# Summing four half rows with one product: the ada rows of a two-block transformer kernel

## The chip, the cores and the metric

The kernel runs on one core of a Trainium2 chip. The metric is the device time of one execution in microseconds (us), lower is better. The engines are named as in the profile: PE is TensorE's matmul, PEld its weight load, DVE is VectorE, ACT is ScalarE, POOL is GpSimd and SP is SyncE, which here issues nearly all DMA transfers; "SPq" marks its queue. A transfer is carried out by 16 DMA engines, which cut it into packets.

## What is computed

The reference runs two transformer blocks over 512 tokens of width 1024. What matters here is the second block's conditioning, computed once for each of its two layers, and the first block's feed-forward part, during which the kernel computes it:

```
def hybrid_layer_2(x, c_act, positions, norm_w, w_ada, b_ada, w_in, ...):
    mod = c_act @ w_ada + b_ada                 # (1,1024) @ (1024,3072)
    shift, scale, gate = jnp.split(mod, 3, axis=-1)
    h = rmsnorm(x, norm_w) * (1.0 + scale[:, None, :]) + shift[:, None, :]
    ...
    return x + gate[:, None, :] * (merged @ w_out)

def second_block(x, c, ...):
    c_act = jax.nn.silu(c)
    ...
def hybrid_layer(x, ...):                        # the first block's end
    ...
    f_gate, f_up = jnp.split(hf @ w_ffn_in, 2, axis=-1)
    f = (jax.nn.silu(f_gate) * f_up) @ w_ffn_out
    return x + rms_norm(f, g_post_ffn)
```

So six rows of 1024 numbers are wanted, three for each layer: shift, scale and gate. Each is a product of one vector with a matrix of 1024 x 1024; all six weight matrices together are 25 MB.

## The kernel before

The large products are made in pairs of fp32r numbers: a weight tile `wr` (128x1024, 512 KB) is loaded by SP (L191, two buffers), ACT rounds it to `wh` (L144), DVE subtracts to get the rest `wl` (L145), each in four buffers and a fifth from another pool, and PE makes three products for each 128 rows: high with high, high with low, low with high. A weight tile of the feed-forward stage (FFN) gives 24 products of 128x128 with 128x512.

The FFN's first half has 44 such tiles. `F_many` makes the first five in halves of 256 tokens and the other 39 whole; I call these 39 the full tiles. After each tile, `done(i, ps)` turns PSUM into `f`: for even i a tanh on ACT and a product on DVE (`ft`, L755), for odd i a product (L759) and a split into high and low (L147 on ACT, L148 on DVE).

The ada rows are computed beside this. `done` starts the generator `ada` when i is 0. A row of 1024 is made as two half rows of 512, so there are twelve half rows. For each one:
- DVE clears an accumulator `acc` (128x512, L573) and SP loads the half row of `b_ada` into its first partition (L574);
- eight times, SP loads a weight tile `aw`: 128 rows of 512 numbers, 256 KB, five buffers (L577), and DVE adds `aw` times a column of `cact` to `acc` (L578). `cact` holds the conditioning vector after silu, 128 numbers in each of eight columns;
- ACT and DVE split `acc` into high and low (L144, L145), and PE sums over the partitions with two products against a 128x128 matrix of ones (`onesr`);
- ACT copies the first row of the result, adding 1.0 for the scale rows (L586), and SP stores it to `ada_rows` in device memory (L587).

The generator yields the time after which its next step is due, by a clock of the program's own that counts PE's products; `tick` in `F_` takes the next step of the generator whose due time has passed. So the pace, 1.2 per `aw` tile, decides where the steps stand among the FFN's products. Within `load_w` a higher priority moves the steps of the weight tiles ahead. In the end each engine has one fixed order, and each works through its own in order. `next_norm` reads two of the rows later, when the second block's normalisation is prepared.

Of the kernel before, what the change touches and what calls it, by code (L numbers as in the profile page):

```python
# [7 lines left out]
F32 = mybir.dt.float32  # L8
F32R = mybir.dt.float32r
I32 = mybir.dt.int32  # L10
AF = mybir.ActivationFunctionType
ALU = mybir.AluOpType
# [3 lines left out]
P = 128  # L16
# [34 lines left out]
class Block:  # L51
# [313 lines left out]
    def run(self):  # L365
        tc, nc, A = self.tc, self.nc, self.A
        with ExitStack() as es:
            self.es = es
            pool = lambda name, **kw: es.enter_context(tc.tile_pool(name=name, bufs=kw.pop("bufs", 1), **kw))
            self.cp = pool("const")  # L370
            self.smp = pool("small", bufs=12)
            self.es_ps = None
            self.psum(ps=8)
            self.hp = pool("h")
            self.dp = pool("dram", space=bass.MemoryType.DRAM)
            self.ident = self.cp.tile([P, P], F32, name="ident")
            self.ones = self.cp.tile([P, P], F32, tag="ones", name="ones")
            self.eps = self.cp.tile([P, 1], F32, tag="eps", name="eps")
            nc.vector.memset(self.eps, EPS)
            nc.scalar.activation(self.sm(), self.eps, AF.Sqrt)  # L380
            nc.vector.memset(self.ones, 1.0)
            self.cact = self.cp.tile([P, 8], F32, tag="cact", name="cact")
            self.xd = [self.dp.tile([S, D], F32, tag=f"xd{i}", name=f"xd{i}") for i in range(3)]
            self.block2(*self.block1())
            self.es_ps.close()
# [168 lines left out]
        v.tensor_add(self.merged[i], self.merged[i], T)  # L554


    def ada_init(self):
        nc, A = self.nc, self.A
        c = self.const("c_2")
        nc.scalar.activation(self.cact, c, AF.Tanh, scale=0.5)  # L560
        nc.vector.scalar_tensor_tensor(self.cact, self.cact, 1.0, c, op0=ALU.add, op1=ALU.mult)
        nc.vector.tensor_scalar(self.cact, self.cact, 0.5, None, op0=ALU.mult)
        self.ada_rows = self.dp.tile([6, D], F32, tag="adar", name="adar")

    def ada(self, pool, pace):

        nc, A, v = self.nc, self.A, self.nc.vector
        ones = pool.tile([P, P], F32R, tag="ones", name="onesr")
        nc.scalar.activation(ones, self.ones, AF.Copy)
        for l, j in [(l, j) for l in range(2) for j in range(6)]:  # L570
            o = slice(j * 512, j * 512 + 512)
            acc = pool.tile([P, 512], F32, tag="acc", name=self.nm("acc"), bufs=2)
            v.memset(acc, 0.0)  # L573
            nc.sync.dma_start(out=acc[0:1, :], in_=A["b_ada_2"][l:l + 1, o])  # L574
            for k in range(8):
                w = pool.tile([P, 512], F32, tag="aw", name=self.nm("aw"), bufs=5)
                nc.sync.dma_start(out=w, in_=A["w_ada_2"][l, k * P:(k + 1) * P, o])  # L577
                v.scalar_tensor_tensor(acc, w, self.cact[:, k:k + 1], acc, op0=ALU.mult, op1=ALU.add)  # L578
                yield pace
            hi, lo = (pool.tile([P, 512], F32R, tag="acc" + c, name=self.nm("acc"), bufs=1) for c in "hl")  # L580
            self.split(hi, lo, acc)
            yield 7.0
            ps = self.pst()
            self.mm(ps, ones, hi, True, False)
            self.mm(ps, ones, lo, False, True)
            nc.scalar.activation(acc[0:1], ps[0:1], AF.Copy, bias=1.0 if j // 2 == 1 else 0.0)  # L586
            nc.sync.dma_start(out=self.ada_rows[l * 3 + j // 2:l * 3 + j // 2 + 1, (j % 2) * 512:(j % 2) * 512 + 512], in_=acc[0:1])  # L587


    def rnn_init(self):  # L590
# [148 lines left out]
    def ffn(self, hf, fp, es_w):  # L739
        tc, nc, A, v = self.tc, self.nc, self.A, self.nc.vector  # L740
        f, th = [], {}
        es = ExitStack()
        pool = []

        def done(i, ps):
            if i == 0:
                self.wait()
                es_w.close()
                pool.append(es.enter_context(tc.tile_pool(name="ffnt", bufs=1, side="right", reuse_waits="tile")))
                self.ada_init()  # L750
                self.spawn(self.ada(pool[0], 1.2))
            if i % 2 == 0:
                t = pool[0].tile([P, S], F32, tag="ft", name=self.nm("ft"), bufs=3)
                nc.scalar.activation(t, ps, AF.Tanh, scale=0.5)
                v.scalar_tensor_tensor(t, t, 1.0, ps, op0=ALU.add, op1=ALU.mult)  # L755
                th[0] = t
            else:
                t = th[0]
                v.tensor_mul(t, t, ps)  # L759
                ft_ = fp.tile([P, 2, S], F32R, tag="f", name=self.nm("f"), bufs=22)  # L760
                self.split(ft_[:, 0, :], ft_[:, 1, :], t, scale=0.5)
                f.append(ft_)

        self.F_many(hf, [A["w_ffn_in"][j * 22 + i] for i in range(22) for j in range(2)], done, halves=5)
        self.wait()
        es.close()
        flat = lambda: fp.tile([P, 2, S], F32R, tag="f", name=self.nm("f"), bufs=22).rearrange("p a q -> p (a q)")
        return lambda k, t, lo: f[k][:, lo, t * P:(t + 1) * P], lambda: [(flat(), flat()) for _ in range(4)]


    def next_norm(self, l, op, pool):

        nc, A, v = self.nc, self.A, self.nc.vector
        if l == 2:
            fin = self.row(A["final_norm_w_2"], pool, "amul")

            halves = []

            def first(t, x):

                xn = pool.tile([P, D], F32, tag="xn", name=self.nm("xn"), bufs=4)
                ms = self.sm()
                nc.scalar.activation(xn[:, :512], x[:, :512], AF.Square, scale=1.0 / 32.0, accum_out=ms)
                v.tensor_mul(xn[:, :512], x[:, :512], fin[:, :512])
                halves.append((xn, self.plus_eps(ms)))

            def more(t, x, a, b):

                xn, e = halves[t]
                ms = self.sm()  # L790
                nc.scalar.activation(xn[:, a:b], x[:, a:b], AF.Square, scale=1.0 / 32.0, accum_out=ms)
                if b < D:
                    v.tensor_mul(xn[:, a:b], x[:, a:b], fin[:, a:b])
                    e2 = self.sm(2)[:, :1]
                    v.tensor_add(e2, e, ms)
                    halves[t] = xn, e2
                    return
                r = self.rsqrt_act(ms, e)
                o = self.out[t * P:(t + 1) * P, :]
                v.scalar_tensor_tensor(xn[:, a:], x[:, a:], r, fin[:, a:], op0=ALU.mult, op1=ALU.mult)  # L800
                nc.sync.dma_start(out=o[:, a:], in_=xn[:, a:])
                nc.scalar.activation(xn[:, :a], xn[:, :a], AF.Copy, scale=r)
                nc.scalar.dma_start(out=o[:, :a], in_=xn[:, :a])

            def last(t, x):
                more(t, x, 512, D)
                yield 0.0

            last.more = more
            last.first = first  # L810
            return last
        nw = self.row(A["norm_w_2"][l], pool, "xn", bufs=2)
        am = self.row(self.ada_rows[l * 3 + 1], pool, "amul")
        sh = self.row(self.ada_rows[l * 3], pool, "ashift")
        v.tensor_mul(am, am, nw)

        def cb(t, x):
            nc.sync.dma_start(out=self.xd[l + 1][t * P:(t + 1) * P, :], in_=x)
            yield from self.norm_T(x, t, op, am, pool, shift=sh, lag=2.0)

        return cb
# [718 lines left out]
def cols(vec, n=None):  # L1540

    return np.ascontiguousarray(vec.reshape(-1, P).T)


def prep(inp):

    f = np.float32
    I = {k: np.asarray(a) for k, a in inp.items()}
    o = {}
    w = I["w_in"][0]  # L1550
# [3 lines left out]
    i = np.arange(P)  # L1554
    m = np.zeros((P, 512), f)
# [3 lines left out]
    n = np.arange(32)  # L1559
# [21 lines left out]
    rows = [cw[0], cw[1], cw[2], cw[3], I["rnn_conv_b"][0], I["rnn_ba"][0], I["rnn_bx"][0], I["rnn_lam"][0]]  # L1581
    o["rnn_cols"] = np.ascontiguousarray(np.stack([cols(r) for r in rows], 1))
    rw = np.zeros((8, P, 2, P), f)
    for j, nme in enumerate(("rnn_wa", "rnn_wx")):
        for h in range(16):
            q = (h % 2) * 64
# [36 lines left out]
    o["w2_out"] = np.stack([packT(I["w_out_2"][l]) for l in range(2)])  # L1623
    o["norm_w_2"], o["final_norm_w_2"] = I["norm_w_2"], I["final_norm_w_2"]
    o["ret_gn"] = np.stack([cols(I["ret_gn_w_2"][l]) for l in range(2)])
    o["c_2"] = cols(I["c_2"][0])
    o["w_ada_2"], o["b_ada_2"] = I["w_ada_2"], I["b_ada_2"]
    w2 = I["nsa_wk2"][0].reshape(2, P, 64).transpose(1, 0, 2)
    o["nsa_wk2"] = np.ascontiguousarray(np.concatenate([w2, w2], 2))
# [24 lines left out]
```

## Time and profile before

| what | before |
|---|---|
| time, median of 3 runs | 2517.1 us (2516.03 to 2517.49) |
| the profiled execution | 2515.06 us |
| its span, first to last instruction | 2513.3 us |
| PE busy | 2493.3 us, 99% of the span |
| DVE busy | 1403.6 us, 56% |
| ACT busy | 1062.7 us, 42% |
| DMA, mean rate over the span | 114 GB/s |
| `aw` loads | 96 of 256 KB, 3.9 us from issue to landing |

The rows come from one profiled execution. A busy row gives time, share of the span and number of instructions. Rows of the timeline give the start, the time and the number of instructions in a row; PE's products overlap, so the step from one start to the next is what one costs. Waits are put down to what came last. In the DMA view, packets under 512 B are counted apart.

### The profile page before, as it was taken

The page shows a single profiled execution, that of the slowest core. Times are in us where ns is not written, and L with a number is a line of the kernel's source. Part 1 is how long each engine was busy: PE and PEld are TensorE (multiplying, and loading weights), DVE is VectorE, ACT ScalarE, POOL GpSimd, SP SyncE. Part 2 cuts the span into 40 slices and gives each one's busy share as a digit, 9 for nine tenths or more (in the row PEclk, how much of TensorE's full clock was granted, in tenths as well). Part 3 has the DMA queues.
Part 4 walks back from the last instruction along what each step waited for, and adds up shares of the span by engine and source line. Part 5 has one row for each costly group of instructions (what it writes and reads, how often), then busy time and mean ns, then how long its engine had stood idle before and what let it go on. Part 6 is the DMA issues. An engine that isn't in the chain of part 4 may idle for free.

```text
span 2513.3 us, 31228 instructions
## 1 busy us (share of the span) xinstructions
PE 2493.3 (99%) x11850; PEld 2056.5 (82%) x11850; DVE 1403.6 (56%) x2651; ACT 1062.7 (42%) x1829; POOL 99.2 (4%) x104
## 2 busy tenths in 40 slices
PE   9999999999999999999999999999999999999998
PEld 7877777878888888888888888888888888888887
DVE  6567665776656777626333436664452343375635
ACT  4477666875334333324343432323233334233323
POOL 0023332000000000000000000000000000000000
PEclk9999999999999999999999999999999999999999
DMA  5522222323345666534422122222443222322233
GB/s 181 173 80 78 70 71 93 95 88 110 118 131 182 211 194 216 184 132 142 134 93 92 62 90 82 86 76 92 144 141 126 89 79 68 101 70 98 68 100 118
DMA packets 99129, 286.47 MB, mean 114 GB/s; under 512 B 13193, under 2 KB 19209, under 8 KB 98850
## 3 DMA queue, kind: packets, MB, share of 16 engines
q1 hardware_dynamic: 98256, 283.22, 35.2%
q8 instruction: 93, 1.52, 0.3%
q10 hardware_dynamic: 722, 1.25, 0.1%
q14 instruction: 58, 0.48, 0.1%
HBM read 259.16 MB, written 12.61 MB: 108 GB/s over the span
## 4 chain that ended last, share of the span: by engine, by line
PE 92%; DVE 3%; ACT 2%; DMA 2%; issue 1%; POOL 0%; ACTq 0%; POOLq 0%; DVEq 0%
PE ps L129 89%; PE ps L138 3%; DMA wr<-in_w_out_dram 1%; DVE wl L145 1%; ACT S L1416 1%; ACT wh L144 0%; DMA wr<-in_w_o_dram 0%; DVE yr L145 0%; POOL S L1423 0%; DVE PTl L145 0%; DVE S L1410 0%; ACT S L1421 0%; DMA x<-in_x_dram 0%; DVE xc L629 0%; DMA wr<-in_nsa_wv_dram 0%
## 5 line engine op out<-in xcount | busy, mean ns | idle before, releaser
L129 PE MATMUL ps<-h,wh 128*128 128x512 f32 (+1 forms) x4000 | 1242.8, 391 | 0.0
L129 PEld LDWEIGHTS ps<-h,wh 128*128 128x128 f32 x4000 | 733.5, 188 | 139.3 <-issue 5.1
L145 DVE TENSOR_TENSOR wl<-wr,wh 128x1024 fp32r<-128x1024 f32 x383 | 469.1, 1225 | 556.1 <-ACT wh L144 555.2
L144 ACT ACTIVATE wh<-wr 128x1024 fp32r<-128x1024 f32 x383 | 405.6, 1059 | 871.4 <-PE ps L129 658.3
L129 PE MATMUL ps<-h,wl 128*128 128x512 f32 (+1 forms) x2000 | 772.9, 386 | 0.0
L129 PEld LDWEIGHTS ps<-h,wl 128*128 128x128 f32 x2000 | 375.9, 188 | 75.7 <-DVE wl L145 0.4
L129 PE MATMUL ps<-wh,h 128*128 128x512 f32 x832 | 261.2, 392 | 0.3 <-ACT h L144 0.3
L129 PEld LDWEIGHTS ps<-wh,h 128*128 128x128 f32 x832 | 156.6, 188 | 33.6 <-DVE h L145 0.8
L129 PE MATMUL ps<-wl,h 128*128 128x512 f32 x416 | 162.4, 390 | 0.0
L129 PE MATMUL ps<-y,wh 128*128 128x512 f32 x384 | 119.3, 391 | 0.0
L129 PEld LDWEIGHTS ps<-wl,h 128*128 128x128 f32 x416 | 78.4, 188 | 16.1
L129 PE MATMUL ps<-wh,f 128*128 128x512 f32 x288 | 89.6, 389 | 0.0
L129 PEld LDWEIGHTS ps<-y,wh 128*128 128x128 f32 x384 | 71.5, 188 | 14.4
L129 PE MATMUL ps<-yr,wh 128*128 128x512 f32 x256 | 78.8, 389 | 0.0
L1416 ACT ACTIVATE S<-S,sm 128x128 f32<-128x128 f32 (+3 forms) x128 | 70.2, 550 | 19.0 <-DVE sm L1414 18.8
L1423 POOL TENSOR_SCALAR S<-S,sm 128x128 f32<-128x128 f32 (+3 forms) x64 | 69.6, 1099 | 214.0 <-ACT Q L144 78.2
L145 DVE TENSOR_TENSOR PTl<-ps,PTh 128x512 fp32r<-128x512 f32 (+1 forms) x96 | 65.0, 683 | 22.4 <-ACT PTh L144 21.6
L144 ACT ACTIVATE PTh<-ps 128x512 fp32r<-128x512 f32 (+1 forms) x96 | 56.1, 588 | 49.0 <-PE ps L138 44.0
L129 PE MATMUL ps<-y,wl 128*128 128x512 f32 x192 | 74.7, 389 | 0.0
L578 DVE SCALAR_TENSOR_TENSOR acc<-aw,cact,acc 128x512 f32<-128x512 f32 x96 | 71.8, 748 | 4.7 <-DMA acc<-in_b_ada_dram 2.7
L1014 DVE CUSTOM_DVE_ANT_0 P<-ps,c_masks 128x128 f32<-128x128 f32 (+1 forms) x96 | 31.2, 325 | 65.0 <-PE ps L129 62.9
L1410 DVE CUSTOM_DVE_ANT_0 S<-ps,c_mask 128x128 f32<-128x128 f32 (+3 forms) x128 | 59.9, 482 | 8.6 <-PE ps L129 7.5
(337 smaller groups left out, 3047.9 us busy)
## 6 DMA issues: line engine op xcount, KB each, us to landing
aw<-in_w_ada_dram SPq DMA_DIRECT2D x96, 256.0 KB, 3.9
wr<-in_w_qk_dram SPq DMA_DIRECT2D x48, 512.0 KB, 3.5
wr<-in_w_ffn_in_dram SPq DMA_DIRECT2D x44, 512.0 KB, 3.8
wr<-in_w_g_dram SPq DMA_DIRECT2D x32, 512.0 KB, 3.5
wr<-in_w_qr_dram SPq DMA_DIRECT2D x32, 512.0 KB, 3.6
wr<-in_w_mg_dram SPq DMA_DIRECT2D x24, 512.0 KB, 3.6
wr<-in_w_va_dram SPq DMA_DIRECT2D x24, 512.0 KB, 4.6
wr<-in_w_ffn_out_dram SPq DMA_DIRECT2D x22, 512.0 KB, 3.9
```

What stands on the lines that cost most here:

```text
L129: self.nc.tensor.matmul(out, a, b, start=start, stop=stop, skip_group_check=True)
L138: self.nc.tensor.transpose(out, in_, self.ident[:k, :k])
L144: nc.scalar.activation(hi, src, AF.Copy)
L145: nc.vector.tensor_sub(lo, src, hi.bitcast(F32))
L578: v.scalar_tensor_tensor(acc, w, self.cact[:, k:k + 1], acc, op0=ALU.mult, op1=ALU.add)
L1014: v.tensor_tensor_reduce(dst, pv, mask, 1.0, -3e38, ALU.add, ALU.max, mx[:, n:n + 1])
L1410: v.tensor_tensor_reduce(Pt[:, o], ps[:, o], self.mask[:, 512 - N:], 1.0, -3e38, ALU.add, ALU.max, mx[:, h:h + 1])
L1416: nc.scalar.activation(Ps[h], Ps[h], AF.Exp, scale=0.125, bias=nm_[:, h:h + 1], accum_out=ls[:, h:h + 1])
L1423: nc.gpsimd.tensor_scalar(Ps[h], Ps[h], r[:, h:h + 1], None, op0=ALU.mult)
```

## The change

The half rows are now taken four at a time, in three groups. A weight tile `aw` holds 32 rows of four half rows: partitions 0 to 31 belong to the first half row, 32 to 63 to the second, and so on. `cact` holds the vector 32 numbers to a column, in 32 columns, repeated for the four quarters. After 32 steps on DVE the accumulator holds four half rows, and PE sums each over its 32 partitions with a 128x4 matrix that has ones in four blocks (`four`, from a new input). So there are 3 splits, 3 pairs of products, 3 evictions and 3 stores instead of 12 of each, and still 96 steps on DVE. The first and the third group lie within one layer and load a tile in one transfer; the second takes two half rows from each layer and loads a tile in two transfers of 64 partitions. The four `b_ada` half rows go to partitions 0, 32, 64 and 96.

`c_2`, `cact` and `four` now live in the FFN's pool, and the vector's silu is computed at the FFN's start instead of the program's. The 1.0 of the scale row is added in `next_norm`. The pace is 1.9 per tile. Of the lines of `fill_up` nothing more is said: they keep addresses as they were.

```
-    def ada_init(self):
-        nc, A = self.nc, self.A
-        c = self.const("c_2")
+    def ada_init(self, pool):
+        nc = self.nc
+        c, self.cact = (pool.tile([P, 32], F32, tag=n, name=n) for n in ("c_2", "cact"))
+        nc.sync.dma_start(out=c, in_=self.A["c_2"])
         nc.scalar.activation(self.cact, c, AF.Tanh, scale=0.5)
...
     def ada(self, pool, pace):
...
-        ones = pool.tile([P, P], F32R, tag="ones", name="onesr")
-        nc.scalar.activation(ones, self.ones, AF.Copy)
-        for l, j in [(l, j) for l in range(2) for j in range(6)]:
-            o = slice(j * 512, j * 512 + 512)
+        four = pool.tile([P, 4], F32, tag="four", name="four")
+        nc.sync.dma_start(out=four, in_=A["four"])
+        ones = pool.tile([P, 4], F32R, tag="ones", name="onesr")
+        nc.scalar.activation(ones, four, AF.Copy)
+        rows = self.ada_rows.rearrange("r (a c) -> (r a) c", c=512)
+        for q in range(3):
             acc = pool.tile([P, 512], F32, tag="acc", name=self.nm("acc"), bufs=2)
             v.memset(acc, 0.0)
-            nc.sync.dma_start(out=acc[0:1, :], in_=A["b_ada_2"][l:l + 1, o])
-            for k in range(8):
+            runs = [(0, 0, 0, 4)], [(0, 4, 0, 2), (1, 0, 2, 2)], [(1, 2, 0, 4)]
+            for l, j, i, n in runs[q]:
+                for m in range(n):
+                    nc.sync.dma_start(out=acc[32 * (i + m):32 * (i + m) + 1, :],
+                                      in_=A["b_ada_2"][l:l + 1, (j + m) * 512:(j + m) * 512 + 512])
+            for k in range(32):
                 w = pool.tile([P, 512], F32, tag="aw", name=self.nm("aw"), bufs=5)
-                nc.sync.dma_start(out=w, in_=A["w_ada_2"][l, k * P:(k + 1) * P, o])
+                for l, j, i, n in runs[q]:
+                    nc.sync.dma_start(out=w[32 * i:32 * (i + n), :], in_=A["w_ada_2"][l, k * 32:k * 32 + 32, j * 512:(j + n) * 512]
+                                      .rearrange("r (j c) -> j r c", j=n))
                 v.scalar_tensor_tensor(acc, w, self.cact[:, k:k + 1], acc, op0=ALU.mult, op1=ALU.add)
                 yield pace
...
             ps = self.pst()
-            self.mm(ps, ones, hi, True, False)
-            self.mm(ps, ones, lo, False, True)
-            nc.scalar.activation(acc[0:1], ps[0:1], AF.Copy, bias=1.0 if j // 2 == 1 else 0.0)
-            nc.sync.dma_start(out=self.ada_rows[l * 3 + j // 2:l * 3 + j // 2 + 1, (j % 2) * 512:(j % 2) * 512 + 512], in_=acc[0:1])
+            self.mm(ps[:4], ones, hi, True, False)
+            self.mm(ps[:4], ones, lo, False, True)
+            nc.scalar.activation(acc[:4], ps[:4], AF.Copy)
+            nc.sync.dma_start(out=rows[4 * q:4 * q + 4, :], in_=acc[:4])
...
-                self.ada_init()
-                self.spawn(self.ada(pool[0], 1.2))
+                self.ada_init(pool[0])
+                self.spawn(self.ada(pool[0], 1.9))
...
-        v.tensor_mul(am, am, nw)
+        v.scalar_tensor_tensor(am, am, 1.0, nw, op0=ALU.add, op1=ALU.mult)
```

The source of an `aw` load was 128 rows of 512 numbers, a row every 3072 numbers. Now it is four blocks, 512 numbers apart, of 32 rows every 3072 numbers, of 512 numbers each; in the middle group it is two such blocks for each of two transfers. The destination is 128 (or 64) partitions of 512 numbers as before.

On SP's queue, in the FFN before, a stretch with two `wr` loads reads:

```order
L191 DMA wr_8465<-in_w_ffn_in_dram 128x1024
L577 DMA aw_8380<-in_w_ada_dram 128x512
L577 DMA aw_8399<-in_w_ada_dram 128x512
L577 DMA aw_8408<-in_w_ada_dram 128x512
L577 DMA aw_8483<-in_w_ada_dram 128x512
L191 DMA wr_8520<-in_w_ffn_in_dram 128x1024
```

In the changed kernel's middle group, also on SP's queue, it reads as follows ("x2" is two transfers in a row for one tile):

```order
L191 DMA wr_8676<-in_w_ffn_in_dram 128x1024
L587 DMA aw_8775<-in_w_ada_dram 64x1x512 x2
L587 DMA aw_8788<-in_w_ada_dram 64x1x512 x2
L191 DMA wr_8722<-in_w_ffn_in_dram 128x1024
L587 DMA aw_8801<-in_w_ada_dram 64x1x512 x2
L587 DMA aw_8824<-in_w_ada_dram 64x1x512 x2
L587 DMA aw_8837<-in_w_ada_dram 64x1x512
L191 DMA wr_8765<-in_w_ffn_in_dram 128x1024
L587 DMA aw_8837<-in_w_ada_dram 64x1x512
```

The `wr` loads still stand between the `aw` loads, two to five tiles apart. There are 30 `wr` loads between the first and the last `aw` load of the changed kernel.

On DVE, this is how the last of the twelve half rows ends before (L578 are the steps of an accumulator, L145 a `wl` or the split of `acc`):

```order
L578 SCALAR_TENSOR_TENSOR acc_9700<-aw_9758,cact,acc_9700 128x512
L145 TENSOR_TENSOR wl_9845<-wr_9842,wh_9844 128x1024
L755 SCALAR_TENSOR_TENSOR ft_9647<-ft_9647,ps_9612 128x512
L578 SCALAR_TENSOR_TENSOR acc_9700<-aw_9767,cact,acc_9700 128x512
L578 SCALAR_TENSOR_TENSOR acc_9700<-aw_9776,cact,acc_9700 128x512
L759 TENSOR_TENSOR ft_9647<-ft_9647,ps_9656 128x512
L145 TENSOR_TENSOR wl_9875<-wr_9872,wh_9874 128x1024
```

And this is how the last of the three groups ends on DVE now; `wl_9390` belongs to the 32nd full tile:

```order
L589 SCALAR_TENSOR_TENSOR acc_9197<-aw_9620,cact,acc_9197 128x512
L589 SCALAR_TENSOR_TENSOR acc_9197<-aw_9632,cact,acc_9197 128x512
L766 SCALAR_TENSOR_TENSOR ft_9164<-ft_9164,ps_9135 128x512
L145 TENSOR_TENSOR wl_9346<-wr_9343,wh_9345 128x1024
L589 SCALAR_TENSOR_TENSOR acc_9197<-aw_9655,cact,acc_9197 128x512
L589 SCALAR_TENSOR_TENSOR acc_9197<-aw_9667,cact,acc_9197 128x512
L589 SCALAR_TENSOR_TENSOR acc_9197<-aw_9679,cact,acc_9197 128x512
L589 SCALAR_TENSOR_TENSOR acc_9197<-aw_9701,cact,acc_9197 128x512
L770 TENSOR_TENSOR ft_9164<-ft_9164,ps_9173 128x512
L145 TENSOR_TENSOR wl_9390<-wr_9387,wh_9389 128x1024
```

The 96 steps stand in DVE's order in another density: one or two to a full tile in tiles 2 to 5, four or five in tiles 6 to 11, two or three in tiles 12 to 24, four or five in tiles 26 to 32, none after. On PE the three pairs stand where the fourth, the eighth and the twelfth pair stood; the order of all other products is unchanged.

## Rows read from the trace of the kernel before

**Rows 1.** The page's head: span; busy us (share of the span) and instructions by engine.
```profile
span 2513.3 us, 31228 instructions
...
PE 2493.3 (99%) x11850; PEld 2056.5 (82%) x11850; DVE 1403.6 (56%) x2651; ACT 1062.7 (42%) x1829; POOL 99.2 (4%) x104
```

**Rows 2.** Chain of waits, 780 to 1080 us: start, length, what. Its last piece.
```profile
821.16 259.05 PE ps L129 x1212
```

**Rows 3.** Waits of SP's queue, 838 to 1060 us: total, times, longest.
```profile
SPq L191 <- DVE wl L145: 64.7, 39, 5.4
SPq L577 <- DVE acc L578: 53.7, 81, 3.2
```

**Rows 4.** PE's timeline: start, length, operation; first full tile, first and twelfth pair.
```profile
838.62 0.63 PE L129 MATMUL ps<-h,wh 128*128 128x512 f32 x2
...
857.01 0.62 PE L129 MATMUL ps<-acc,onesr 128*128 128x512 f32 x2
857.46 0.62 PE L129 MATMUL ps<-h,wh 128*128 128x512 f32 x2
...
1055.80 0.62 PE L129 MATMUL ps<-acc,onesr 128*128 128x512 f32 x2
```

**Rows 5.** PE's groups by shape, whole span: count, busy us, mean ns, idle before.
```profile
L138 PE MATMUL ps<-ident,S 128*128 128x128 f32 x320 | 50.3, 275 | 1.1 <-POOL S L1423 1.1
...
L129 PE MATMUL ps<-acc,onesr 128*128 128x512 f32 x24 | 7.4, 389 | 0.0
...
L129 PE MATMUL ps<-row,one 1*128 1x512 f32 x4 | 3.7, 1089 | 3.1 <-DMA row<-in_g_pre_mix_dram 3.1
...
L138 PE MATMUL ps<-ident,mc 128*4 128x128 f32 x8 | 1.2, 272 | 0.0
```

**Rows 6.** DMA view of 861.7 to 863.2, of 858.5 to 861.5, of 840 to 1056.
```profile
DMA packets 2, 0.00 MB, mean 1 GB/s; under 512 B 1, under 2 KB 1, under 8 KB 2
...
DMA packets 136, 0.49 MB, mean 162 GB/s; under 512 B 17, under 2 KB 17, under 8 KB 136
...
DMA packets 17767, 42.94 MB, mean 199 GB/s; under 512 B 1989, under 2 KB 1989, under 8 KB 17754
...
aw<-in_w_ada_dram SPq DMA_DIRECT2D x83, 256.0 KB, 3.7
wr<-in_w_ffn_in_dram SPq DMA_DIRECT2D x34, 512.0 KB, 4.2
wr<-in_w_ffn_out_dram SPq DMA_DIRECT2D x6, 512.0 KB
adar<-acc SPq DMA_DIRECT2D x11, 2.0 KB
acc<-in_b_ada_dram SPq DMA_DIRECT2D x10, 2.0 KB
```

**Rows 7.** Tiles `aw` and `W`: ns of one, min/median/max, first and last start.
```profile
L577 SPq DMA_DIRECT2D aw<-in_w_ada_dram x96: 327/328/1061, 813.7 to 1038.3; - x96
L578 DVE SCALAR_TENSOR_TENSOR acc<-aw,cact,acc x96: 628/751/754, 823.1 to 1043.1; 128x512 f32<-128x512 f32 x96
...
L1471 SPq DMA_DIRECT2D W<-Z x16: 591/602/650, 143.5 to 432.2; - x16
```

**Rows 8.** Windows: busy us by engine, clock, DMA share, GB/s; then 850:856 in slices.
```profile
840.00:1056.00 216.00, 216.00 (x954) 178.88 (x953) 157.88 (x208) 72.91 (x100) 0.00 (x0) 1.00 0.62 199
850.00:856.00 6.00, 6.00 (x28) 4.99 (x27) 2.91 (x4) 2.11 (x4) 0.00 (x0) 1.00 0.83 277
...
GB/s 355 273 410 273 314 246 273 259 314 341 355 341 355 246 300 273 355 355 369 437 355 396 232 287 328 328 369 273 300 300 300 219 273 191 137 137 109 82 0 0
```

**Rows 9.** SP's timeline: the loads at the FFN's start.
```profile
818.28 7.41 SPq L577 DMA_DIRECT2D aw<-in_w_ada_dram  x7
```

**Rows 10.** DVE's timeline: one split of `wl` and one `ft` step.
```profile
850.65 1.23 DVE L145 TENSOR_TENSOR wl<-wr,wh 128x1024 fp32r<-128x1024 f32 x1 [0.25 <-ACT wh L144]
851.79 0.68 DVE L755 SCALAR_TENSOR_TENSOR ft<-ft,ps 128x512 f32<-128x512 f32 x1
```

More of the change, by code (lines that the diff above doesn't have):

```diff
@@ L381, in run @@
             nc.vector.memset(self.ones, 1.0)
-            self.cact = self.cp.tile([P, 8], F32, tag="cact", name="cact")
+            self.fill_up(self.cp, 64)
             self.xd = [self.dp.tile([S, D], F32, tag=f"xd{i}", name=f"xd{i}") for i in range(3)]
@@ L562, in ada_init @@
         nc.vector.tensor_scalar(self.cact, self.cact, 0.5, None, op0=ALU.mult)
+        self.fill_up(pool, 224)
         self.ada_rows = self.dp.tile([6, D], F32, tag="adar", name="adar")
@@ L1625, in prep @@
     o["ret_gn"] = np.stack([cols(I["ret_gn_w_2"][l]) for l in range(2)])
-    o["c_2"] = cols(I["c_2"][0])
+    o["c_2"] = np.ascontiguousarray(np.tile(I["c_2"][0].reshape(32, 32).T, (4, 1)))
+    o["four"] = np.repeat(np.eye(4, dtype=f), 32, axis=0)
     o["w_ada_2"], o["b_ada_2"] = I["w_ada_2"], I["b_ada_2"]
```

## The prediction

> **What bounds the kernel now.** I read the page's head first: the span is 2513.3 us and TensorE (PE) is busy for 2493.3 us of it, 99% [rows 1]. The profiled execution took 2515.06 us, 2.0 us under the median of 2517.1. So a removed product is worth its slot, and everything else is worth nothing unless PE comes to wait. Next I looked at the place of the change. The chain of waits is one unbroken piece of PE work there: 259.05 us from 821.16, 1212 products [rows 2]. The feed-forward stage (FFN) is thus PE-bound from end to end, and the ada rows ride along on SP's queue, VectorE (DVE) and ScalarE (ACT). They ride on shared queues, though. SP stands 53.7 us at `aw` transfers and 64.7 us at `wr` transfers, each time until DVE has freed a buffer [rows 3]. SP and DVE work in order, so a late `aw` makes its product on DVE late, the next `wl` behind that, and then PE.
>
> PE's clock of work in this stage comes from its timeline [rows 4]. The first full weight tile starts at 838.62. An ada pair takes 857.46 - 857.01 = 0.45 us, 0.2265 us a product, though one product is listed with 389 ns [rows 5], since they overlap. The 39 full tiles of 24 products plus 11 earlier ada pairs give 838.62 + 39 x 24 x 0.2265 + 11 x 0.453 = 1055.6; the row of the twelfth pair stands at 1055.80. A weight tile is thus 5.44 us.
>
> **PE's part: 18 products fewer.** 24 ada products become 6. If a product with four columns costs the slot of one with 128, the gain is 18 x 0.2265 = 4.08 us. The trace has no `fp32r` product with four columns over 512. The nearest row is a transpose to four columns, 272 ns against 275 ns for one to 128 [rows 5]: no difference, and I take none. The bounds are a free product (6 x 0.2265 = 1.4 us more gain) and the 1089 ns of the start's one-row products [rows 5], 6 x (1.089 - 0.389) = 4.2 us less gain. So PE's own part lies between -5.4 and +0.1 us.
>
> **The rest of the list.** 96 products `acc<-aw,cact,acc` on DVE stay 96. Nine memsets, splits, evictions and row stores go; none is on the chain. The conditioning vector moves from the start into the FFN's head: one small load, an ACT tanh and two small DVE steps. PE works without a gap there [rows 2] on tiles that are loaded, so I cost them at nothing; without cover they would be a few us once. The 1.0 that ACT added moves into a DVE step of the same count.
>
> **The transfers.** This is where I expect the time. Bytes stay the same: 96 tiles of 256 KB. What changes is the form. Before, a transfer's outermost count was 128 rows on both sides. Now the source is 4 x 32 x 512, outermost count 4, for the first and third group; the middle group has two transfers a tile, each 2 x 32 x 512. How does a transfer divide itself? The trace shows it in the packets under 512 B, one of which each share leaves behind its data. Between 861.7 and 863.2 a single 2 KB row moved: 2 packets, 1 small. Between 858.5 and 861.5 one `wr` and one row moved: 17 small, 16 + 1. From 840 to 1056 there are 123 issues of `aw` and `wr` and 21 single rows: 123 x 16 + 21 = 1989, the number shown [rows 6]. So a transfer of 128 rows is cut into 16 shares and one of a single row into 1, and the cut follows the outermost count, not the bytes. No transfer before has an outermost count between 1 and 16. I read the rule on: 4 gives four shares, 2 gives two, and I take them to go to the same, first engines each time. [...] A source of three levels also reaches the queue as such: the `W<-Z` loads take 602 ns to issue where an `aw` takes 328 [rows 7], which for 128 issues, 77 us, is no bound on SP.
>
> [...] No run here shows yet which engines a share of four goes to.
>
> **The price.** A quarter of a tile is 65.5 KB and half of a 128 KB transfer is 65.5 KB too. The first engines carry 32 + 2 x 32 + 32 = 128 such shares, 8.39 MB, where before each carried 96 x 16.4 KB = 1.57 MB. Between the first and the last `aw` stand 30 `wr`, 32.8 KB each per engine, 0.98 MB. The rate of an engine: 199 GB/s at a busy share of 0.62 is 20.1 GB/s an engine; 277 at 0.83 is 20.9; the fastest slice from 850 to 856, 437 GB/s, is 27.3 [rows 8]. The shares of busy time are from all engines competing; with twelve nearly idle I expect more, and take the middle, 23.7. Then 8.39 MB take 354 us and 0.98 MB take 41.5 us. The `aw` loads behind the first `b_ada` row began to leave at 818.28 [rows 9]; with four such rows ahead I start at 820. The last `aw` lands at 820 + 354 + 41.5 = 1215.5. On DVE the last product, 0.75 us [rows 7], and an `ft` step and the split of `wl`, 0.68 and 1.23 us [rows 10], bring it to 1218.2, where PE can start the 32nd full tile, since all 96 products stand before that tile's `wl` (DVE's order). Before, that tile starts at 838.62 + 31 x 5.44 + 9 x 0.453 = 1011.3. The delay is 207 us, and the one pair that remains behind it instead of three gives 0.9 back: **+206 us**. With 27.3 GB/s it is 820 + 307 + 36 + 2.7 - 1011.3 - 0.9 = +154 us, with 20.1 it is +277 us.
>
> Two checks. Do the first engines stay busy? The five `aw` buffers are refilled as products end, and SP stops at a `wr` only until the `wl` two tiles earlier is split, about 1.2 us behind a product, with several `aw` still in flight; so yes. Does PE's clock matter? It is granted 1.00 here [rows 8]. [...]
>
> **Rivals.** *A, sixteen shares after all* (not slower): the cut follows the 128 or 64 partitions of the destination. For it: in every row read, the source's count and the destination's partitions are equal, so the rows don't separate them. Against it: a source that offers only 4 outermost. Then the -4.1 us of PE's part stand: 2513.0, within 2511.7 to 2517.2. DVE's dense tiles, 5 x 0.75 + 1.23 + 0.68 = 5.7 us against 5.44, fall behind by some 2 us in seven tiles, less than one of the four `wl` buffers. It decides from the number of shares: 5.44 us hold 129 KB an engine at 23.7 GB/s, less 32.8 for `wr`, at 4.5 `aw` a tile, 21.4 KB each, which is 12 shares or more. With eight the stage is late already. *C, few shares but on engines in turn*: the load evens out, and only a tile whose shares meet on one engine waits, at most 2.8 us in each of 13 dense tiles: 2513 to 2549. *D, the change doesn't do what it says*, a product of four columns at 1.09 us: it is the +0.1 end of A and hidden by B.
>
> **How the numbers follow.** B, the forecast of four and two shares on the same engines, gets 0.80: the cut by the outermost count is in the rows, the step from 16 and 1 to 4 and 2 is read on. A gets 0.13, C 0.07. B gives 2517.1 + 205.9 = 2723.0 (the profiled execution 2721), from 2671 to 2794 by the two rates. The range is 2650 to 2800: a few engines alone may run somewhat faster than any mean over sixteen, and DVE or SP may leave small gaps. It leaves out A and most of C, 2 in 10. About 0.2%, 5 us, is what a measurement of this kernel can tell from no change. Faster than that needs A with nearly free products: 0.04. Within it lies the rest of A and a part of C, 0.13. Slower is 0.83.
>
> **What would show it.** Right: 4 small packets per `aw` of the outer groups and 2 per transfer of the middle one; `aw` landings of 10 us and more instead of 3.7 [rows 6]; a DMA share of a few tenths while PE waits at `wl`, ended by `aw` products on DVE and `wr` landings; PE idle some 200 us between 840 and 1260. Wrong: 16 small packets each, landings near 4 us and an unbroken PE piece; or four small packets with landings near 5 us (C). If the size is off, it is the rate of one engine, or gaps in which the first engines have nothing queued.

## The result and the profile after

The changed kernel takes 2704.03 us (median of 5 runs, 2701.48 to 2707.36), the kernel before 2516.03 us on the same chip (5 runs, 2513.23 to 2517.49): a ratio of 1.075, 95% interval 1.074 to 1.077, or 188 us more. 2723 us were forecast, with a range of 2650 to 2800 us. The profiled execution of after took 2707.36 us, the slowest of the five.

The page's head and its clock row, for [rows 1]. PE is busy for 56 us more, with 18 products fewer, and its clock (tenths of full speed, 40 slices) is down in five slices in the middle:

```profile
span 2705.6 us, 31138 instructions
...
PE 2548.9 (94%) x11832; PEld 2088.6 (77%) x11832; DVE 1395.3 (52%) x2633; ACT 1053.8 (39%) x1811; POOL 100.5 (4%) x104
...
PEclk9999999999999777779999999999999999999999
```

The FFN's full tiles, for [rows 8]: a window from the first of them to the point where the waits end (busy us and count by engine, then PE's clock, DMA share, GB/s), and what PE and DVE waited for (us, times, longest):

```profile
838.00:1201.00 363.00, 227.90 (x763) 175.50 (x762) 131.52 (x170) 50.74 (x65) 0.00 (x0) 0.79 0.31 108
...
PE ps L129 <- DVE wl L145: 135.1, 25, 8.8
...
DVE acc L589 <- DMA aw<-in_w_ada_dram: 220.5, 83, 4.8
```

PE stands still for 135 us and waits for `wl` each time; DVE, which makes `wl`, stands for 220 us at `aw` loads. The unbroken PE piece of [rows 2] is gone. The 31 tiles and the ada pairs among them (two now, nine before) fill this window of 363 us but for about 1 us, where 31 x 5.44 + 9 x 0.453 = 173 us stood before: some 190 us more. Of these 135 are idle and 55 are products that took longer, in this window at a mean granted clock of 0.79. From 952 to 954 the clock reads 0.50 and products follow each other after 0.43 us, from 956 to 958 it reads 1.00 and they follow after 0.23 us; 49 of the 55 us lie in stretches that read 0.50.

How the loads run is seen best in stretches in which only `aw` moves. The DMA view in slices, GB/s: first 866 to 876, in the first group, where a `wr` begins in the last slice; then 1007 to 1017, in the middle group, with one `wr` in it:

```profile
GB/s 98 107 98 98 98 106 98 115 98 107 107 107 115 82 123 98 90 98 106 98 115 98 98 106 98 98 98 107 98 115 98 106 98 98 98 107 98 107 106 328
...
GB/s 57 57 49 49 49 49 49 49 57 57 49 197 131 180 246 426 328 451 287 41 41 49 49 57 49 49 49 49 57 49 49 57 49 49 49 49 57 49 57 57
```

Where `aw` runs alone the rate is flat at about 102 GB/s in the one and 51 GB/s in the other. The middle group has two transfers to a tile and up to five tiles on their way, and still moves half as much: the transfers share the same engines. The packets of SP's queue in the trace, counted at every moment, say the same: from 936 to 1088 never fewer than two are under way, and exactly two for 116 of the 152 us; from 1110 to 1198 there are fewer than four for only 0.4 us. So the few engines hardly ever stood idle. When a `wr` comes, the busy share of the 16 engines goes from one tenth to nine and the slices to 426 and 451. The packets under 512 B, for [rows 6], from 840 to 1230:

```profile
DMA packets 17361, 43.70 MB, mean 112 GB/s; under 512 B 976, under 2 KB 976, under 8 KB 17348
...
wr<-in_w_ffn_in_dram SPq DMA_DIRECT2D x35, 512.0 KB
aw<-in_w_ada_dram SPq DMA_DIRECT2D x56, 256.0 KB
aw<-in_w_ada_dram SPq DMA_DIRECT2D x64, 128.0 KB
wr<-in_w_ffn_out_dram SPq DMA_DIRECT2D x3, 512.0 KB
acc<-in_b_ada_dram SPq DMA_DIRECT2D x6, 2.0 KB
adar<-acc SPq DMA_DIRECT2D x2, 8.0 KB
```

With 16 for each `wr`, 4 for an `aw` of 256 KB and for a store of four rows, 2 for an `aw` of 128 KB and 1 for a single row, that is 38 x 16 + 56 x 4 + 64 x 2 + 2 x 4 + 6 = 974 of the 976. So here a transfer with 4 outermost was cut into four shares and one with 2 into two, and not every transfer is carried out by all 16 engines. The rates agree: 102 GB/s are 4 x 25.5, 51 are 2 x 25.5. Which of the sixteen engines they are, no run here shows.

The end of the stage, on DVE's timeline and then on PE's, for [rows 4, 10]; then the last two long pieces of the chain of waits from 780 to 1320:

```profile
1195.73 0.75 DVE L589 SCALAR_TENSOR_TENSOR acc<-aw,cact,acc 128x512 f32<-128x512 f32 x1 [1.73 <-DMA aw<-in_w_ada_dram]
1198.26 0.75 DVE L589 SCALAR_TENSOR_TENSOR acc<-aw,cact,acc 128x512 f32<-128x512 f32 x1 [1.77 <-DMA aw<-in_w_ada_dram]
1198.92 0.68 DVE L770 TENSOR_TENSOR ft<-ft,ps 128x512 f32<-128x512 f32 x1
1199.52 1.22 DVE L145 TENSOR_TENSOR wl<-wr,wh 128x1024 fp32r<-128x1024 f32 x1
...
1200.79 0.79 PE L129 MATMUL ps<-h,wl 128*128 128x512 f32 x1 [4.09 <-DVE wl L145]
...
1184.71 13.45 DMA aw<-in_w_ada_dram
1200.79 119.23 PE ps L129 x512
```

A product on DVE follows the one before it after 2.5 us, the time of one share of 65.5 KB at 26 GB/s. The last of the 96 stands at 1198.26, `wl` follows, and PE goes on at 1200.79; from there on it never stops again in this stage. That last `aw` took 13.45 us from its issue to its landing, where 3.7 us was the median before [rows 6].

### The profile page after: what moved, and what is told of

It reads as the page before. It is cut to its first block, busy times and chain, and to the rows that moved or that the text cites. A ratio compares the mean times of both kernels' runs of the same rounds, so it can differ in the third digit from the quotient of the medians.

```text
span 2705.6 us, 31138 instructions
## 1 busy us (share of the span) xinstructions
PE 2548.9 (94%) x11832; PEld 2088.6 (77%) x11832; DVE 1395.3 (52%) x2633; ACT 1053.8 (39%) x1811; POOL 100.5 (4%) x104
## 4 chain that ended last, share of the span: by engine, by line
PE 79%; DMA 11%; DVE 3%; SPq 3%; ACT 3%; issue 1%; POOL 0%; DVEq 0%; ACTq 0%; POOLq 0%
PE ps L129 76%; DMA aw<-in_w_ada_dram 9%; PE ps L138 3%; SPq L587 2%; DVE wl L145 1%; DMA wr<-in_w_out_dram 1%; ACT S L1427 1%; ACT wh L144 1%; DMA wr<-in_w_ffn_in_dram 1%; SPq L191 0%; DMA wr<-in_w_o_dram 0%; DVE acc L589 0%; DVE yr L145 0%; POOL S L1434 0%; ACT S L1432 0%
## 5 line engine op out<-in xcount | busy, mean ns | idle before, releaser
L129 PE MATMUL ps<-h,wh 128*128 128x512 f32 (+1 forms) x4000 | 1277.9, 400 | 0.0
L129 PE MATMUL ps<-h,wl 128*128 128x512 f32 (+1 forms) x2000 | 799.1, 400 | 135.1 <-DVE wl L145 135.1
L129 PEld LDWEIGHTS ps<-h,wh 128*128 128x128 f32 x4000 | 759.2, 195 | 148.5 <-issue 5.4
L145 DVE TENSOR_TENSOR wl<-wr,wh 128x1024 fp32r<-128x1024 f32 x383 | 469.1, 1225 | 563.8 <-ACT wh L144 561.5
L129 PEld LDWEIGHTS ps<-h,wl 128*128 128x128 f32 x2000 | 389.0, 195 | 225.2 <-DVE wl L145 146.0
L145 DVE TENSOR_TENSOR PTl<-ps,PTh 128x512 fp32r<-128x512 f32 (+1 forms) x96 | 65.1, 684 | 22.1 <-ACT PTh L144 21.3
```

The costliest lines, as they stand in the source:

```text
L129: self.nc.tensor.matmul(out, a, b, start=start, stop=stop, skip_group_check=True)
L145: nc.vector.tensor_sub(lo, src, hi.bitcast(F32))
```

## The experiments

**One thing undone: the outermost count.** The four half rows are interleaved over the partitions, so that the source runs over 32 rows first. The columns of the vector and the block matrix are permuted to match; number and order of the instructions are those of the changed kernel, on every engine.

```
-                    nc.sync.dma_start(out=w[32 * i:32 * (i + n), :], in_=A["w_ada_2"][l, k * 32:k * 32 + 32, j * 512:(j + n) * 512]
-                                      .rearrange("r (j c) -> j r c", j=n))
+                    nc.sync.dma_start(out=w[32 * i:32 * (i + n), :], in_=A["w_ada_2"][l, k * 32:k * 32 + 32, j * 512:(j + n) * 512]
+                                      .rearrange("r (j c) -> r j c", j=n))
...
-    o["four"] = np.repeat(np.eye(4, dtype=f), 32, axis=0)
+    o["four"] = np.concatenate([np.eye(4, dtype=f)[p % 4], np.eye(4, dtype=f)[p // 64 * 2 + p % 2]], 1)
```

> The changed kernel with one thing undone, the outermost count: the four half rows are interleaved over the partitions (partition 4r+m, in the middle group 2r+m of each half), so that the source runs over 32 rows first and reads 8 KB or 4 KB from each. The columns of the vector and the block matrix are permuted to match. Number and order of the instructions on SP, ACT, DVE and PE are those of the changed kernel, unlike with four loads a tile. Theory (the outermost count sets the engines): 16 small packets per transfer, PE without a gap, the 18 products saved: 2511 us, 2508 to 2516. Rival (the order and density of the 96 steps on DVE and SP): above 2650 us. Rival (a source of several levels is slow as such): slower than 2560 us.

Measured: 2510.71 us against 2513.49 us, ratio 0.9988, interval 0.9979 to 0.9997. The whole loss of 188 us is gone, and the kernel is faster than the one before by 2.8 us (0.8 to 5.3). The chain of this kernel from 780 to 1080, two pieces of its PE timeline, its issue row of `aw`, and its packets from 840 to 1056:

```profile
821.15 258.97 PE ps L129 x1211
...
911.40 0.63 PE L129 MATMUL ps<-acc,onesr 128*4 128x512 f32 x2
911.87 0.62 PE L129 MATMUL ps<-h,wh 128*128 128x512 f32 x2
...
1051.80 0.63 PE L129 MATMUL ps<-acc,onesr 128*4 128x512 f32 x2
...
L587 SPq DMA_DIRECT2D aw<-in_w_ada_dram x128: 528/541/1917, 818.6 to 982.1; - x128
...
DMA packets 18847, 44.09 MB, mean 204 GB/s; under 512 B 2563, under 2 KB 2563, under 8 KB 18834
```

PE's piece is whole again. From 840 to 1056, 161 transfers of 128 or 64 rows are issued (118 of them `aw`), three stores of four rows and six single rows. With 16 small packets for each of the 161 that is 161 x 16 + 3 x 4 + 6 = 2594, and 2563 are counted; with 4 and 2 for the `aw` it would be 1050. So the `aw` run on sixteen engines here. With order and density as in the changed kernel, the rival that blames these is out, and so is the one that blames a source of several levels: an issue still takes 541 ns, not the 328 of the plain pattern [rows 7], and costs nothing. One more thing changes with this edit: the source is now read in runs of 8 or 4 KB instead of 2 KB. That is not the cure, since the kernel before reads runs of 2 KB without a loss. The PE rows also price the products: a pair with four columns takes 911.87 - 911.40 = 0.47 us, where one with 128 took 0.45 [rows 4]. Four columns save nothing over 128, and the 1.09 us of rival D is out. The last pair stands at 1051.80 instead of 1055.80: 4.0 us for 18 products.

**The groups apart.** In both kernels one kind of group reads from a copy of the weights that lies in tiles (128 or 64 rows outermost, given as a further input), the other is left as changed; the order of instructions is the changed kernel's.

```
+                    src = (A["w_pack"][q, k, 32 * i:32 * (i + n), :] if q == 1 else
+                           A["w_ada_2"][l, k * 32:k * 32 + 32, j * 512:(j + n) * 512].rearrange("r (j c) -> j r c", j=n))
```

> The changed kernel with the middle group alone reading from a copy of the weights that lies ready in tiles, so that its transfers have 64 rows outermost; the order of instructions is that of the changed kernel. The outer groups keep four engines. Theory: each outer group needs (32 x 65.5 + 11 x 32.8 KB) / 25 GB/s = 98 us where PE has work for 60; about 21 us are lost in the first and 36 in the third group: 2567 us, 2550 to 2590. Rival (order): 2700 us.

> The counterpart: the outer groups read 128 rows outermost, the middle group keeps two engines. Theory: it needs (64 x 65.5 + 13 x 32.8 KB) / 25 GB/s = 185 us where PE has work for some 92 from the first load to the tile that waits for the last: 2603 us, 2585 to 2625. So the middle group costs about 1.6 times what the two outer ones cost together. Rival (order): 2700 us.

Measured: 2587.18 us with the middle group cured and 2605.04 us with the outer ones cured (one run each), 76 and 94 us above the kernel that has all three cured. Windows of the first of them, then of the second (columns as above):

```profile
880.00:940.00 60.00, 40.51 (x144) 31.91 (x145) 34.26 (x46) 13.44 (x17) 0.00 (x0) 0.79 0.54 170
940.00:1000.00 60.00, 60.00 (x266) 49.46 (x265) 41.52 (x55) 17.63 (x24) 0.00 (x0) 1.00 0.67 204
1000.00:1060.00 60.00, 39.94 (x136) 30.77 (x135) 24.56 (x32) 8.67 (x12) 0.00 (x0) 0.80 0.35 126
...
820.00:880.00 60.00, 60.00 (x343) 52.98 (x342) 48.87 (x66) 21.91 (x29) 0.00 (x0) 1.00 0.73 242
...
940.00:1000.00 60.00, 30.88 (x96) 23.46 (x96) 16.79 (x23) 6.70 (x9) 0.00 (x0) 0.74 0.23 81
...
1060.00:1120.00 60.00, 58.44 (x254) 46.79 (x253) 53.03 (x68) 22.32 (x31) 0.00 (x0) 1.00 0.72 240
```

PE is full in the stretch of the cured group and waits in that of the other, at a lower clock each time. Both times lie in their ranges: the middle group was placed well (2603 expected), the outer ones cost 20 us more than expected (2567). The ratio of the two is 1.2, not 1.6. The sum, 171 us, is under the 191 us (188.0 + 2.8) that lie between the changed kernel and the one with all three cured. A likely reason, argued and not measured: behind a cured group the prefetch has a lead again that the next slow group uses up first.

**The form put into the kernel before.** Here nothing but the source's pattern changes: the 128 rows of a tile are taken as 4 blocks, or 8 blocks, of every fourth or eighth row, and the vector is permuted to match.

```
-                nc.sync.dma_start(out=w, in_=A["w_ada_2"][l, k * P:(k + 1) * P, o])
+                nc.sync.dma_start(out=w, in_=A["w_ada_2"][l, k * P:(k + 1) * P, o].rearrange("(r j) c -> j r c", j=4))
```

> The kernel before with one thing changed: the source of a weight load is written as 4 blocks of 32 rows (every fourth row of the same 128; the vector is permuted to match), so its outermost count is 4. Order and counts are as before. Theory: four engines carry 96 x 65.5 KB and about 36 x 32.8 KB, 7.5 MB, at the 25 GB/s an engine that the changed kernel showed (102 GB/s flat on four): 300 us from 814, the last tile lands near 1115, the last pair of products starts near 1118 instead of 1056: about 2577 us, 2555 to 2600. Rival (order and pace are the cause): 2516 us.

> As the last one, with 8 blocks of 16 rows: outermost count 8. Theory: eight engines carry 96 x 32.8 KB and 36 x 32.8 KB, 4.3 MB, 174 us, which fits into the 240 us that the rows have: 2516 us, within 5; 8 small packets per transfer. Rival (any three-level source is slow, whatever the number of shares): as slow as the one with four, 2555 us or more.

Measured: 2645.88 us with four (one run) and 2541.82 us with eight (ratio 1.011, interval 1.009 to 1.013), against 2514.29 us. More engines, less loss, and the order before with four engines is slow too: that much speaks for the number of engines. Both sizes were missed, by 69 and by 26 us. The packets and the waits of this stage, first with four, then with eight:

```profile
DMA packets 17365, 44.13 MB, mean 130 GB/s; under 512 B 1008, under 2 KB 1008, under 8 KB 17352
...
DVE acc L573 <- DMA adar<-acc: 94.0, 9, 12.5
...
DVE acc L578 <- DMA aw<-in_w_ada_dram: 58.9, 30, 3.7
...
PE ps L129 <- ACT acc L144: 49.4, 8, 21.7
...
DMA packets 15836, 39.24 MB, mean 178 GB/s; under 512 B 1211, under 2 KB 1211, under 8 KB 15823
...
DVE acc L573 <- DMA adar<-acc: 52.8, 9, 7.4
...
PE ps L129 <- ACT acc L144: 16.9, 2, 13.1
```

The small packets fit 4 and 8 for an `aw`: 85 x 4 + 40 x 16 + 20 = 1000 against 1008, and 80 x 8 + 35 x 16 + 19 = 1219 against 1211.

I had added up bytes as if the engines were always fed. They aren't here: a new half row clears an accumulator whose row must first be stored (L573), a store that is itself late, and until then SP stands at the half row of `b_ada`, with the next `aw` behind it. With eight blocks SP stood there for 60.1 us in ten waits; with four it issued nothing from 1000.80 to 1010.88, and no data moved from about 1011.9 to 1013.6. The changed kernel has that chain three times, this one twelve times.

> The kernel before with 8 blocks a load, which lost 27 us, and four accumulators instead of two. Theory: what was lost there is the chain of one half row to the next: a new accumulator waits for the store of the row two before it, and that row of 2 KB waits in the queue of the engine that also carries the eighths; with four accumulators the wait on the store goes: 2518 us, 2510 to 2525. Rival (eight engines are too few for the loads): stays at 2535 to 2550 us.

The edit is `bufs=4` for `acc` instead of 2. Measured: 2538.46 us in one run, where the four runs with two accumulators lie between 2538.49 and 2546.51: no gain that one run could tell. The 2518 us that my theory gave for these 27 us were missed. The wait on the store only went from 52.8 to 28.6 us, and PE's waits from 22 to 14. Nor is the run a clean split: with four accumulators the order moved too, and from the third half row on the `aw` loads on SP and their products on DVE stand two to seven weight tiles earlier. So the store is neither shown to cost the 27 us nor cleared of it; that its 2 KB wait on an engine that also carries eighths was my theory, and no run shows it. In stretches the eight engines run at a flat rate (some 210 GB/s, 8 x 26, from 1015 to 1017 with two accumulators) and stand idle in others (next to nothing moved from about 1001.7 to 1004.7). Which link of that chain costs the 27 us stays open.

**Four loads a tile.** These two came first, and one assumption in them was wrong, that the order of instructions would stay. A tile is loaded by four transfers of 32 rows, in all groups or in the middle one alone:

```
+                    for m in range(n):
+                        nc.sync.dma_start(out=w[32 * (i + m):32 * (i + m) + 32, :],
+                                          in_=A["w_ada_2"][l, k * 32:k * 32 + 32, (j + m) * 512:(j + m) * 512 + 512])
```

> Only the form of the weight loads is undone: each tile is loaded by four transfers of 32 rows, outermost count 32 on both sides, everything else as in the changed kernel. Theory (a transfer is shared out by its outermost count, and four or two engines carry the tiles): 16 small packets per transfer, no wait of PE at the weight tiles, and PE's own saving of 18 products is left: about 2512 us, 2510 to 2517. Rival (the place of the 96 steps in DVE's and SP's order, denser by stretches, is what makes the tiles late): stays above 2650 us. Rival (SP's issue time): 384 issues at 0.33 us are 127 us in 195 us, so a little lost at most, 2515 to 2530.

> The changed kernel with the middle group alone loaded by transfers of 32 rows; the outer groups keep the outermost count 4. Theory: an outer group takes (32 x 65.5 + 11 x 32.8 KB) / 25 GB/s = 98 us for 60 us of PE work; about 20 us are lost in the first and 30 in the third, none in the middle: about 2560 us, 2540 to 2580, so the middle group with its two engines makes up some 140 of the 188 us. Rival (order): above 2650 us.

Measured: 2662.61 us (ratio 1.059, interval 1.057 to 1.061) and 2600.56 us (one run); both forecasts, 2512 and 2560, were missed. Taken alone, the first would have felled my theory. But its waits are others (838 to 1250, then the landing times of `aw`):

```profile
ACT ft L766 <- PE ps L129: 140.2, 20, 9.9
...
PE ps L129 <- ACT wh L144: 59.9, 29, 3.0
...
DVE acc L590 <- DMA aw<-in_w_ada_dram: 3.5, 2, 2.7
...
DMA to landing us min/median/max: 1.7/2.4/4.5
```

The loads are fast (2.4 us), hardly anything waits for them (3.5 us), and PE waits for ACT instead. On ACT's timeline each `wh` stands behind an `ft` or `f`, which waits for PE, the `f` by way of DVE's `ft`:

```profile
1008.81 0.60 ACT L766 ACTIVATE ft<-ps 128x512 f32<-128x512 f32 x1 [8.63 <-PE ps L129]
1009.30 1.05 ACT L144 ACTIVATE wh<-wr 128x1024 fp32r<-128x1024 f32 x1
1019.30 0.63 ACT L147 ACTIVATE f<-ft 128x512 fp32r<-128x512 f32 x1 [8.96 <-DVE ft L771]
1019.84 1.04 ACT L144 ACTIVATE wh<-wr 128x1024 fp32r<-128x1024 f32 x1
```

With 384 loads instead of 128 the order itself had changed: counted in ACT's order, `wh` stands four to five tiles later among the `ft` and `f` than in the changed kernel, so the lead of the weights is gone. That the number of loads on SP's queue is what moved them is argued, from the fact that nothing else differs. The run shows that the tiles can land fast and the stage still be slow; whether the number of engines made the changed kernel slow, it can't decide. In the second kernel the order shifts in the same way from the middle group on, so it is no clean split either. That is why the three kernels above were made to keep the order.

## Why the prediction was right

**What bounds, and where the time goes.** Right. The loss is in the named stretch, and in the named chain: `aw` late, its product on DVE late, `wl` behind it, PE waits.

**Four and two shares, on the same engines.** Right, and now measured rather than read on: the small packets (974 of 976), the flat 102 and 51 GB/s, the 13.45 us of an `aw` landing, and the kernel that puts 32 rows outermost with every instruction in its place. No row of before shows a cut into four or two. That the shares go to the first engines, as the sum has it, no run shows; that they go to the same ones, the 51 GB/s of the middle group show. Rival A (sixteen shares) and rival C (engines in turn) are both out for this form. A's price was good: 4.0 us of PE work, 2.8 us measured for the kernel that has it.

**The rate.** The term that was off. 23.7 GB/s an engine was a choice, the middle between 20.1 and 27.3 [rows 8], and no row of before favoured it; that it came this near was partly luck. Where `aw` runs alone an engine moves 25.5 GB/s (102 / 4, 51 / 2). The 9.37 MB took from 819 to 1198, 379 us instead of 395, 24.7 GB/s with the `wr` in between. That gives PE's restart at 1200.8 instead of 1218.2, a delay of 189.5 us instead of 207, less 0.9 for the pairs: 188.6, and 188.0 by the medians.

**PE idle for 200 us.** Wrong as put. It is 135 us idle and 55 us of longer products, 49 of them at a granted clock of 0.50. The prediction has the clock at 1.00 [rows 8]; it was 0.79 in the mean from 838 to 1201. That did not move the end, since data set the pace: between 850.94 and 1200.79 the long pieces of the chain of waits are `aw` landings, issues on SP and `wl`, and none is PE's. The check that the few engines stay busy was right (from 936 to 1088 never fewer than two packets under way); but the idle time a reader should look for was too high, and part of the loss hides in PE's busy time.

**SP.** Wrong: "77 us, is no bound". The price of the pattern itself was good (with sixteen engines an issue takes 0.541 us in the median, some 69 us for 128), but in the changed kernel an issue of `aw` took 2.04 us in the median, not 0.6, and all 128 took 228 us. In the middle group SP's issues stand on the chain of waits between the `aw`. No loss of its own can be told apart, as the few engines had packets under way all that time.

**Decision point of rival A.** "With eight the stage is late already" held (27 us), in the kernel before and for a reason that stays partly open.

## What to carry to other kernels

When a load's source is rearranged, look at its outermost count before its bytes: in this case 4 blocks of 32 rows ran on four engines and 32 rows of 4 blocks on sixteen (2704.03 against 2510.71 us, with the middle group changed alike), with the same bytes and the same number of instructions. The partition layout was free here, since a permuted vector and block matrix undo the interleaving; such freedom is best spent on the loads. And an experiment that changes the number of instructions on a queue may change the order on other engines as well; the order has to be compared before the times are.

## What the runs showed of the hardware beside that

Where the few engines were behind, SP's queue was held up at its issues, 2.04 us each in the median. The `aw` issue on SP after, for [rows 7], and a piece of SP's timeline after:

```profile
L587 SPq DMA_DIRECT2D aw<-in_w_ada_dram x128: 521/2040/5185, 819.2 to 1184.7; - x128
...
1137.24 11.42 SPq L587 DMA_DIRECT2D aw<-in_w_ada_dram  x5
1148.71 0.99 SPq L191 DMA_DIRECT2D wr<-in_w_ffn_in_dram  x1
1150.46 12.78 SPq L587 DMA_DIRECT2D aw<-in_w_ada_dram  x5
```

The median went from 0.33 to 2.04 us, and five issues take 11 to 13 us, 2.3 to 2.6 us each: about the time in which an engine moves one share of 65.5 KB. With the same number of issues and all sixteen engines (32 rows outermost) the median was 0.54 us. So SP did not only wait for buffers, as before; the issue itself took about that time, and a `wr` behind it left later too.

PE's clock is the other thing. A window of the middle group in the changed kernel, PE's waits in it, and a window behind the stage:

```profile
911.00:1061.00 150.00, 88.05 (x268) 66.65 (x269) 44.63 (x58) 19.62 (x25) 0.00 (x0) 0.75 0.25 87
...
PE ps L129 <- DVE wl L145: 66.7, 12, 8.8
...
1250.00:1300.00 50.00, 50.00 (x222) 41.38 (x222) 12.26 (x10) 9.55 (x9) 0.00 (x0) 1.00 0.47 158
```

The granted clock has a mean of 0.75 where PE stood still for 62 of 150 us (the twelve waits are 67 us with what lies outside the window), and it is back at 1.00 from 1250 to 1300, where PE works through. Where PE had no such waits, in the kernel before and in the one with 32 rows outermost, it is 1.00 from 840 to 1056.
